# Attention's value projection moved ahead of attention as seven half-size block products

## The chip, the cores and the metric

The kernel runs on one core of a Trainium2 chip. Its time is the device time of one execution in microseconds (us), and lower is better. The engines are named as in the profile: PE is the matrix engine (PEld its weight loads), DVE the vector engine, ACT the scalar engine, POOL the GpSimd engine, and SP the queue that issues nearly all DMAs.

## The reference

A trunk of two layers works on a sequence of 1024 tokens of width 1024 in float32. The second layer mixes tokens by differential attention with 8 heads; cut to what matters here:

```python
q, k, v = jnp.split(hn @ w_qkv, 3, axis=-1)          # hn = rms_norm(h): 1024 x 1024; w_qkv: 1024 x 3072
q = rms_norm(q.reshape(b, s, 8, 2, 64), q_gain) * 64 ** -0.5
k = rms_norm(k.reshape(b, s, 8, 2, 64), k_gain)
v = v.reshape(b, s, 8, 128)
logits = einsum('bqhrd,bkhrd->bhrqk', q, k) - slopes * dist      # slopes[hd] = 2 ** -(hd + 1), causal mask
probs = softmax(logits)
o = einsum('bhqk,bkhe->bqhe', probs[:, :, 0] - lam * probs[:, :, 1], v)
h = h + (rms_norm(o, sub_gain) * (1 - lam_init)).reshape(b, s, 1024) @ w_out
```

The value projection is thus one product of 1024 x 1024 by 1024 x 1024. After attention come a wide MLP and a gated embedding, as in the first layer.

## The kernel before, in words

Matrix products keep float32 accuracy by splitting each operand into a high and a low part (`split`, L228 to L238: a cast on ACT at L230, a subtraction at L234) and multiplying three times (`mm3`, L206): high by high, high by low, low by high. So one product step of 128 contraction rows is three PE instructions.

The stages run in this order: the mixer of the first layer, an MLP, a gate called `ple`, then `attention`, then its output projection, a second MLP and a second gate, `ple_out`. In `mlp` and `ple_out` a large product is already done as seven products of half-size blocks with additions of the operands beside them. The inputs of attention are the 16 pairs of `hs`: the transposed activations times their norm's gain, high and low, for 8 slices of channels by two halves of 512 tokens. The norm's factor per token, `r`, is multiplied in later.

In `attention` PE work comes from two sources. The blocks: for each head `hd` and each block `b` of 128 queries (64 blocks in all) a `Block` makes logits (`qk`, against the keys `ks`), a DVE instruction that adds the distance bias `al` and takes the running minimum (L1132), an exponential on ACT (L1135), a combination of the two softmaxes on DVE (`combine`, L1141 to L1143), transposes (`tr`) copied back by ACT (`aT`, L1153), and the product with the values (`po`, L1160). The blocks are staggered: combination one block later, transposes and values two blocks later. The other source is the fill: a generator `fill` of projections. Each `next(fill)` emits one unit of 12 PE instructions, 128x256 each; a projection of a head's queries and keys has 16 units, half of one of a pair of heads' values has 8. That makes 128 units for queries and keys and 64 for values. 24 units come before the first block. The rest are spread over 264 calls of `pump`, four per block, by the table `MARKS` (call number, units by then): 168 units by call 226. Output projection parts (`tail`) follow from call 210 on.

Value units take weights through SP into `raw`, split them (the cast on ACT, the subtraction on POOL for projections) and leave the product through ACT (`proj_v`, L1049), which scales by `r` and writes a tile for two heads. For each head the queries are transposed and split by `put_q`: ACT writes the high part of one half of the partitions (L1091), DVE copies it to the other half (L1092) and makes the low part (L1093). The bias: slopes halve from head to head, so each block first halves its newest 128 columns of `al` on DVE (L1118).

A scheduler with a cost model of its own sets the order in which each engine gets its instructions; names, priorities and dependencies are what the code gives it.

Of the kernel before, what the change touches and what calls it, by code (L numbers as in the profile page):

```python
# [11 lines left out]
F32 = mybir.dt.float32  # L12
F32R = mybir.dt.float32r
AF = mybir.ActivationFunctionType
ALU = mybir.AluOpType
# [28 lines left out]
def f32(ap):  # L44
    return ap.bitcast(F32)
# [73 lines left out]
class Trunk:  # L119
# [581 lines left out]

    def ple_out(self, pT, acc, gain, wg, wpj, out):
        nc = self.nc
        o = out.rearrange("(t p) f -> p t f", p=P)
# [249 lines left out]

    def attn_consts(self, q_gain, k_gain, lam, sub_gain, lam_init):
        nc, cp = self.nc, self.cp
        qg = cp.tile([P, 1], F32, name="qg")
        kg = cp.tile([P, 1], F32, name="kg")  # L960
        for t, a in ((qg, q_gain), (kg, k_gain)):
            for i in range(2):
                nc.sync.dma_start(t[64 * i : 64 * (i + 1), :], a.rearrange("(p o) -> p o", o=1))
        nc.vector.tensor_scalar(kg, kg, 8.0, None, ALU.mult)
# [17 lines left out]
    def attention(self, w_qkv, w_out, gain_next, h_dram):  # L982

        nc = self.nc
        NB = NT
# [57 lines left out]
        def proj_v(pr, hf, out):  # L1043
            def evac(t2, ps):
                if len(out) == pr:
                    out.append(self.slot(f"A{pr % 2}", [P, NT, 256], F32, "v"))
                for i in range(2):
                    t = 2 * t2 + i
                    nc.scalar.activation(out[pr][:, t, :], ps[:, 256 * i : 256 * (i + 1)], AF.Copy, scale=r[t // 4][:, t % 4 : t % 4 + 1])  # L1049

            return proj(f"v{pr}", [w_qkv[:, 2 * D + pr * 256 : 2 * D + (pr + 1) * 256]], (2 * hf, 2 * hf + 1), evac)

        half = (slice(0, 64), slice(64, P))


# [11 lines left out]
        def begin(hd):  # L1067

            qk = qks[hd]

            ks = self.slot(f"A{2 + hd % 2}", [P, 2, S], F32R, "ks")

            def put_k(hf):
                pt = self.aux([P, HT], "tr", "tr")
                for t in range(4):
                    self.pe.transpose(pt[:, t * P : (t + 1) * P], qk[1][hf][:, t, :], self.ident)
                for r in range(2):
                    own, other = half[r], half[1 - r]
                    dst = ks[:, r, hf * HT : (hf + 1) * HT]
                    nc.scalar.activation(dst[own], pt[own], AF.Copy, scale=self.kg[own])  # L1080
                    nc.vector.scalar_tensor_tensor(dst[other], pt[own], self.kg[own], f32(dst[own]), ALU.mult, ALU.subtract)

            def put_q(b2):
                pt = self.aux([P, HT], "tr", "tr")
                for i in range(2):
                    self.pe.transpose(pt[:, i * P : (i + 1) * P], qk[0][b2 // 2][:, 2 * (b2 % 2) + i, :], self.ident)
                qh = self.slot(f"c{11 + b2 % 2}", [P, 2, 2 * P], F32R, "qh")
                ql = qlow[b2 % 2]
                for r in range(2):
                    own, other = half[r], half[1 - r]  # L1090
                    nc.scalar.activation(qh[own, r], pt[own, 0 : 2 * P], AF.Copy, scale=self.qg[own])  # L1091
                    nc.vector.tensor_copy(qh[other, r], f32(qh[own, r]))  # L1092
                    nc.vector.scalar_tensor_tensor(ql[own, r], pt[own, 0 : 2 * P], self.qg[own], f32(qh[own, r]), ALU.mult, ALU.subtract)  # L1093
                return qh, ql

            put_k(0)
            heads[hd] = [ks, put_k, put_q, put_q(0)]

        class Block:
# [12 lines left out]

            def logits(me, r):
                hd, b, n, nm, lg = me.hd, me.b, me.n, me.nm, me.lg[r]
                if r == 0:

                    new = al[:, (NB - 1 - b) * P : (NB - b) * P]
                    inst = nc.vector.tensor_scalar(new, new, 0.5, None, ALU.mult)  # L1118
                    if b:

                        self.pe.behind(inst, self.pe.mark)
# [4 lines left out]
                for c in range(nch):  # L1126
# [3 lines left out]
                    self.pe.matmul(ps[:, : k1 - k0], lhsT=ql[:, r, qs], rhs=ks[:, r, k0:k1], start=False, stop=True)  # L1130

                    nc.vector.tensor_tensor_reduce(  # L1132
                        out=lg[:, k0:k1], in0=ps[:, : k1 - k0], in1=al[:, u0 + k0 : u0 + k1], scale=-1.0,
                        scalar=3.0e38 if c == 0 else nm[:, r, 0:1], op0=ALU.add, op1=ALU.min, accum_out=nm[:, r, c : c + 1])
                nc.scalar.activation(lg[:, :n], lg[:, :n], AF.Exp, bias=nm[:, r, nch - 1 : nch], scale=-1.0, accum_out=me.sums[:, b, r : r + 1])  # L1135

# [77 lines left out]
        for hd in range(1, 8):  # L1214
            projs.append(proj_qk(hd, qks[hd]))
            if hd < 7:
                projs.append(proj_v((hd + 1) // 2, (hd + 1) % 2, vs))
        fill = self.stream(projs)
        for _ in range(24):
            next(fill)  # L1220
        begin(0)

        marks = [(0, 0), *MARKS]
# [2 lines left out]
        def pump():  # L1226
            i = state[0] = state[0] + 1
            for (i0, u0), (i1, u1) in zip(marks, marks[1:]):
                if i0 < i <= i1:
                    want = u0 + (u1 - u0) * (i - i0) / (i1 - i0)  # L1230
                    while state[1] < want:
                        next(fill)
                        state[1] += 1
            if i > TAIL and (state[1] < 168 or i % 4):
                next(tail, None)

        def tails():
            while state[1] < 160:
                yield
            for i in range(KA[0]):  # L1240
                fetch_o(0, i)
            while state[1] < 168:
# [11 lines left out]
        tail = tails()  # L1254
        blocks = []
        for g in range(8 * NB + 2):
            if g < 8 * NB:
# [849 lines left out]
def trunk(tc, x, p, ln_mix_e, w_in_e, gmlp_v_gain, gmlp_ws, gmlp_bs, gdn_conv, gdn_a_log, gdn_dt_bias, gdn_out_gain,  # L2107
          w_out_e, ln_mix_o, w_qkv_o, attn_q_gain, attn_k_gain, diff_lambda, attn_sub_gain, w_out_o, ln_mlp, w_mlp1,
          w_mlp2, ln_ple, w_ple_gate, w_ple_proj, masks, out):
    with ExitStack() as ctx:  # L2110
# [60 lines left out]
        for layer in range(2):  # L2171
# [23 lines left out]
            T.ple(pT, acc, w_ple_gate[0], w_ple_proj[0], gain[3], h_dram)  # L2195
            T.wide = ("mm",)
            T.attention(w_qkv_o[0], w_out_o[0], gain[4], h_dram)


# [39 lines left out]
```

## Time and profile before

| | before |
|---|---|
| timed runs, median (lowest to highest) | 2499.75 us (2499.11 to 2500.47) |
| profiled execution: its span, first to last instruction | 2498.9 us |
| PE, DVE, ACT, POOL busy | 2490.6, 1809.4, 1312.3, 285.6 us |
| the chain that ended last: on PE, on DVE | 96%, 2% |
| granted PE clock | 1.000 |

The page gives no other time of the profiled execution than its span, which is 0.85 us below the median of the timed runs. A row of grouped instructions reads: line, engine, operation, output tile <- input tiles, shape, count | busy us, mean ns of one | idle time of the engine before them and what ended it. The ends of PE's instructions are modelled and overlap, so PE's pace is read from the starts: a row of the chain gives a start, a length and a count. A row of stretches gives, for a stretch of the span, its length and each engine's busy time with the number of instructions.

### The profile page before, as it was taken

What the parts mean: (1) busy time and instruction counts of PE and PEld (TensorE: products, weight loads), DVE (VectorE), ACT (ScalarE), POOL (GpSimd) and SP (SyncE); (2) the same over time, 40 slices, a digit from 0 to 9 for tenths busy, and PEclk for the clock granted to TensorE, in tenths of its full rate; (3) what the DMA queues carried; (4) which work ended last, traced back from release to release, by engine and by line L of the source; (5) the groups of instructions that cost most, each with busy time, mean ns of one, the idle gap of its engine ahead of it and who ended that gap; (6) DMA issues with size and microseconds to landing.
All of it is one profiled execution on the core that took longest, in us unless ns stands there. A gap on an engine that the chain in (4) does not pass through costs nothing.

```text
span 2498.9 us, 39861 instructions
## 1 busy us (share of the span) xinstructions
PE 2490.6 (100%) x13897; PEld 2138.1 (86%) x13897; DVE 1809.4 (72%) x3542; ACT 1312.3 (53%) x2668; POOL 285.6 (11%) x267
## 2 busy tenths in 40 slices
PE   9999999999999999999999999999999999999999
PEld 7898998888888888888999999988888888888887
DVE  7868665787666877656577877777887656788586
ACT  6635473655555444544466666654654555445452
POOL 0211220000000000000444444310000000000000
PEclk9999999999999999999999999999999999999999
DMA  8464435567547756543211111366466548656651
GB/s 236 128 187 107 141 125 172 161 207 241 188 166 272 241 160 213 188 130 132 81 52 60 52 52 60 108 216 223 154 222 221 197 159 295 200 192 200 197 177 64
DMA packets 319506, 411.07 MB, mean 165 GB/s; under 512 B 46308, under 2 KB 182472, under 8 KB 319304
## 3 DMA queue, kind: packets, MB, share of 16 engines
q1 hardware_dynamic: 318744, 408.00, 50.6%
q8 instruction: 109, 1.79, 0.3%
q14 instruction: 93, 0.76, 0.1%
q10 hardware_dynamic: 560, 0.53, 0.1%
HBM read 296.21 MB, written 112.21 MB: 163 GB/s over the span
## 4 chain that ended last, share of the span: by engine, by line
PE 96%; DVE 2%; issue 1%; ACT 0%; DMA 0%; ACTq 0%; DVEq 0%
PE mm L80 84%; PE po L80 3%; PE qk L80 2%; PE aux L80 2%; PE tr L83 2%; DVE lg L1132 1%; DVE lg L1143 0%; DMA x<-in_x_dram 0%; PE pks L80 0%; PE pkq L80 0%; PE pkk L80 0%; PE pvn L80 0%; PE pgm L80 0%; PE pab L83 0%; PE pst L80 0%
## 5 line engine op out<-in xcount | busy, mean ns | idle before, releaser
L230 ACT CAST w<-raw 128x512 fp32r<-128x512 f32 x598 | 366.6, 617 | 463.7 <-PE mm L80 404.2
L80 PE MATMUL mm<-g,w 128*128 128x512 f32 x2592 | 601.6, 394 | 0.0
L80 PEld LDWEIGHTS mm<-g,w 128*128 128x128 f32 x2592 | 486.6, 188 | 113.9
L80 PE MATMUL mm<-hi,w 128*128 128x512 f32 x1728 | 554.5, 396 | 0.0
L80 PE MATMUL mm<-w,hi 128*128 128x256 f32 (+2 forms) x2528 | 507.2, 295 | 0.9 <-DVE k L1034 0.9
L234 DVE TENSOR_TENSOR w<-raw,w 128x512 fp32r<-128x512 f32 x534 | 366.8, 693 | 192.1 <-ACT w L230 180.3
L80 PEld LDWEIGHTS mm<-w,hi 128*128 128x128 f32 x2528 | 401.2, 188 | 13.8 <-issue 1.2
L80 PEld LDWEIGHTS mm<-hi,w 128*128 128x128 f32 x1728 | 324.4, 188 | 73.7 <-ACT u L386 0.4
L80 PE MATMUL mm<-w,lo 128*128 128x256 f32 (+2 forms) x1264 | 370.1, 294 | 0.0
L80 PE MATMUL mm<-lo,w 128*128 128x512 f32 x864 | 340.3, 394 | 0.0
L80 PE MATMUL mm<-t,w 128*128 128x512 f32 x1152 | 271.4, 394 | 0.0
L80 PEld LDWEIGHTS mm<-t,w 128*128 128x128 f32 x1152 | 216.4, 188 | 50.6
L80 PEld LDWEIGHTS mm<-w,lo 128*128 128x128 f32 x1264 | 238.1, 188 | 5.5
L80 PEld LDWEIGHTS mm<-lo,w 128*128 128x128 f32 x864 | 162.5, 188 | 36.2
L275 POOL TENSOR_TENSOR r<-ms,mhalf 128x4 f32<-128x4 f32 x12 | 14.1, 1173 | 1505.1 <-DVE ms L273 1474.5
L234 DVE TENSOR_TENSOR g<-graw,g 128x512 fp32r<-128x512 f32 x216 | 147.7, 686 | 6.6 <-DMA gd<-g 5.8
L230 ACT CAST g<-graw 128x512 fp32r<-128x512 f32 x216 | 132.6, 617 | 23.4 <-DMA gd<-g 7.3
L1135 ACT ACTIVATE lg<-lg,nm 128x256 f32<-128x256 f32 (+7 forms) x128 | 99.2, 776 | 69.1 <-DVE nm L1132 64.2
L370 ACT ACTIVATE g<-g 128x512 f32<-128x512 f32 x100 | 63.0, 631 | 79.5 <-DVE g L304 79.2
L1132 DVE CUSTOM_DVE_ANT_0 lg<-qk,al 128x512 f32<-128x512 f32 (+3 forms) x128 | 74.6, 589 | 36.9 <-PE qk L80 33.2
L234 POOL TENSOR_TENSOR w<-raw,w 128x512 fp32r<-128x512 f32 x64 | 84.1, 1335 | 76.2 <-ACT w L230 58.2
L80 PE MATMUL mm<-ohi,w 128*128 128x512 f32 x256 | 84.3, 400 | 0.0
(360 smaller groups left out, 3574.2 us busy)
## 6 DMA issues: line engine op xcount, KB each, us to landing
raw<-in_w_mlp_dram SPq DMA_DIRECT2D x352, 256.0 KB, 3.3
graw<-gd SPq DMA_DIRECT2D x224, 256.0 KB, 2.7
gd<-g SPq DMA_DIRECT2D x192, 256.0 KB, 3.4
raw<-in_w_ple_gate_dram SPq DMA_DIRECT2D x76, 256.0 KB, 3.5
acc<-h_dram SPq DMA_DIRECT2D x64, 256.0 KB, 4.4
keep<-in_w_mlp_dram SPq DMA_DIRECT2D x64, 256.0 KB, 4.8
raw<-in_w_in_e_dram SPq DMA_DIRECT2D x60, 256.0 KB, 3.6
h_dram<-acc SPq DMA_DIRECT2D x48, 256.0 KB, 3.3
```

Of the source, the lines that this page charges most:

```text
L80: self._next(self.engine.matmul(*a, **k))
L83: self._next(self.engine.transpose(*a, **k))
L230: inst = self.nc.scalar.copy(hi, src)
L234: inst = (lo_engine or self.nc.vector).tensor_tensor(lo, src, f32(hi), ALU.subtract)
L275: nc.gpsimd.tensor_tensor(r, ms, self.mhalf[:, 0:4], ALU.pow)
L370: nc.scalar.activation(g, src, AF.Relu)
L1132: nc.vector.tensor_tensor_reduce(out=lg[:, k0:k1], in0=ps[:, : k1 - k0], in1=al[:, u0 + k0 : u0 + k1], scale=-1.0, scalar=3.0e38 if c == 0 ...
L1135: nc.scalar.activation(lg[:, :n], lg[:, :n], AF.Exp, bias=nm[:, r, nch - 1 : nch], scale=-1.0, accum_out=me.sums[:, b, r : r + 1])
```

## The change

The value projection leaves the fill. A new function `values` runs between `ple` and `attention`. It treats activations and value weights as two by two blocks of 512 (`a11` to `a22` of `hs`, and `w_qkv`'s last 1024 columns) and makes seven products of 512x512x512 after Winograd: `s1` to `s4` are sums of activations, written over the residual stream `acc`, which is in DRAM by then; `t1` to `t4` are sums of weight blocks. Two sets of four PSUM banks, `x` and `y`, collect the products; ACT copies and DVE additions scale by `r` and combine them, and SP stores the results to `v_dram` in 32 pieces. `attention` reads them back as four tiles of two heads each: two before the first head, one each at blocks 18 and 34. The fill holds 128 units, 16 of them before the first block and 112 spread evenly to call 224, a half per call (before about 0.73). The subtractions for value weights, formerly POOL's, are DVE's in `values`.

Two smaller edits in `attention`: `al` is no longer halved; instead the queries' gain of head `hd` is multiplied by 2^(hd+1) and the DVE instruction's scale is -0.5^(hd+1). And ACT writes both halves of a query tile from PSUM; the copy on DVE is gone.

```diff
-MARKS = ((64, 50), (192, 144), (226, 168))
+MARKS = ((224, NQK),)
...
+    def values(self, acc, gain, w_qkv):
...
+        a11, a12, a22 = self.hs[0][0:4], self.hs[0][4:], self.hs[1][4:]
+        v_dram = self.dp.tile([NT, P, D], F32, name="v_dram")
...
+        def product(ps, a, b, new=False):
+            for k in R:
+                for q in R:
+                    self.mm3(ps[q], [y[:, q * P : (q + 1) * P] for y in a[k]], b[k], new and k == 0, k == 3, not new)
...
+        b11 = right(lambda k: raw(0, 0, k))
...
+            tt(t1[k], raw(0, 1, k), raw(0, 0, k), ALU.subtract)
...
+        product(x, a11, b11, True)
+        copies(u, x, 0)
+        b21 = right(lambda k: raw(1, 0, k))
+        for k in R:
+            tt(t2[k], t1[k], raw(1, 1, k), ALU.subtract)
+        product(y, a12, b21, True)
+        close(0, 0, y, u)
+
+        for k in R:
+            nc.scalar.activation(acc[k][1], acc[k][1], AF.Copy, scale=gain[:, k : k + 1])
+            scaled(acc[4 + k][1], 4 + k, 1, acc[k][1], ALU.add)
...
+        s2s = left(("A4", "A5"), s2)
+        t2s = right(lambda k: t2[k])
+        product(x, s2s, t2s)
+        copies(u, x, 0)
...
+        product(y, s1s, t1s, True)
+        copies(t, y, 1)
...
+        product(x, s3s, t3s)
+        close(1, 1, x, t)
...
+        product(y, s4s, b22)
+        close(0, 1, y, u)
...
+        product(x, a22, t4s)
+        close(1, 0, x)
...
-                    nc.scalar.activation(qh[own, r], pt[own, 0 : 2 * P], AF.Copy, scale=self.qg[own])
-                    nc.vector.tensor_copy(qh[other, r], f32(qh[own, r]))
+                    nc.scalar.activation(qh[own, r], pt[own, 0 : 2 * P], AF.Copy, scale=g)
+                    nc.scalar.activation(qh[other, r], pt[own, 0 : 2 * P], AF.Copy, scale=g)
...
-                    inst = nc.vector.tensor_scalar(new, new, 0.5, None, ALU.mult)
...
-        projs = [proj_v(0, 0, vs), proj_qk(0, qks[0]), proj_v(0, 1, vs)]
...
+        fill = self.stream([proj_qk(hd, qks[hd]) for hd in range(8)])
+        for _ in range(16):
             next(fill)
+        values(0)
+        values(1)
```

What stands in the queues differs at three places on which the steps below rest. First PE, behind the last product of `ple` (`aux<-phi`); `hi`, `lo` are the activations of attention, `w` weights, and `aux<-ones,sqs` sums the squares of the second half of the tokens. Before:

```order
L80 MATMUL aux_12167<-phi_8239,wpl_11315 128x512
L80 MATMUL mm_12266<-w_12244,hi_11712 128x256
L80 MATMUL mm_12266<-w_12245,hi_11712 128x256
L80 MATMUL mm_12266<-w_12244,lo_11713 128x256
...
L80 MATMUL aux_12216<-ones,sqs_11841 128x1 x4
```

After (the first row is again the last of `ple`, and `s` is the split `s2`):

```order
L81 MATMUL aux_12175<-phi_8247,wpl_11323 128x512
L81 MATMUL mm_12286<-w_12236,hi_11720 128x512
...
L81 MATMUL mm_12293<-w_12358,lo_11741 128x512
L81 MATMUL aux_12224<-ones,sqs_11849 128x1 x4
L81 MATMUL mm_12287<-w_12236,hi_11720 128x512
...
L81 MATMUL mm_12286<-w_12476,s_12466 128x512
```

Between the last row of `ple` and the sum of squares stand 73 instructions of 128x256 before, 54 of 128x512 now; 42 more of the first two products follow it, and then the third product, which needs `s2`.

Second DVE at the same time, from the last gate's product with `rb` (L671, now L672) to the last sum of squares (`sqs`). Before:

```order
L671 TENSOR_TENSOR t_12174<-mm_12125,rb_11402 128x512
L257 TENSOR_TENSOR sqs_11841<-sqs_11841,t_12164 128x512
L246 SCALAR_TENSOR_TENSOR lo_12209<-acc_8280,cols,hi_12208 128x512
L674 SCALAR_TENSOR_TENSOR t_12177<-t_12174,aux_12167 128x512
L675 SCALAR_TENSOR_TENSOR acc_8280<-t_12177,acc_8280 128x512
L257 TENSOR_TENSOR sqs_11841<-sqs_11841,t_12181 128x512
```

After (`raw` rows make `t3`, `acc` rows from L740 make `s1` to `s4`):

```order
L672 TENSOR_TENSOR t_12182<-mm_12133,rb_11410 128x512
L740 SCALAR_TENSOR_TENSOR acc_8285<-acc_8285,cols,acc_8288 128x512
L258 TENSOR_TENSOR sqs_11849<-sqs_11849,t_12172 128x512
L247 SCALAR_TENSOR_TENSOR lo_12217<-acc_8288,cols,hi_12216 128x512
L740 SCALAR_TENSOR_TENSOR acc_8285<-acc_8285,cols,acc_8288 128x512
L714 TENSOR_TENSOR raw_12666<-raw_12666,raw_12668 128x512
L740 SCALAR_TENSOR_TENSOR acc_8286<-acc_8286,cols,acc_8285 128x512
L675 SCALAR_TENSOR_TENSOR t_12185<-t_12182,aux_12175 128x512
...
L676 SCALAR_TENSOR_TENSOR acc_8288<-t_12185,acc_8288 128x512
...
L258 TENSOR_TENSOR sqs_11849<-sqs_11849,t_12189 128x512
```

Counted from the L674 (now L675) before the last but two to that last sum of squares, DVE had 18 instructions and has 42 now. Third ACT, where a new head begins (`ks` keys, `qh` queries, `lg` the exponentials). Before:

```order
L1080 ACTIVATE ks_16476<-tr_16477,kg 64x512
L1091 ACTIVATE qh_16489<-tr_16486,qg 64x256
L230 CAST w_16308<-raw_16306 128x512
L230 CAST w_16441<-raw_16439 128x512
L1080 ACTIVATE ks_16476<-tr_16477,kg 64x512
L230 CAST w_16591<-raw_16588 128x512
L1091 ACTIVATE qh_16489<-tr_16486,qg 64x256
```

After:

```order
L1188 ACTIVATE ks_16382<-tr_16383,kg 64x512
L1143 ACTIVATE t_16461<-mm_16318 128x512
L1200 ACTIVATE qh_16395<-tr_16392,qg 64x256
L1201 ACTIVATE qh_16395<-tr_16392,qg 64x256
L1237 ACTIVATE lg_12932,sums_15826<-lg_12932,nm_16402 128x1024
L1188 ACTIVATE ks_16382<-tr_16383,kg 64x512
L1200 ACTIVATE qh_16395<-tr_16392,qg 64x256
L1201 ACTIVATE qh_16395<-tr_16392,qg 64x256
```

The casts of weights moved elsewhere, two query copies came in, and an exponential stands between.

More of the change, by code (lines that the diff above doesn't have):

```diff
@@ L32 @@
 KA = (6,5)
[L33 removed]
+NQK = 112
+MARKS = ((224, NQK),)
 TAIL = 210
@@ L980, in attn_consts, with attention @@
         self.qg, self.kg, self.sg, self.nlam = qg, kg, sg, nl
-    def attention(self, w_qkv, w_out, gain_next, h_dram):
+    def attention(self, w_qkv, v_dram, w_out, gain_next, h_dram):
         nc = self.nc
@@ L1211, in attention, with values @@
         qks, vs, os = [[] for _ in range(8)], [], [[] for _ in range(8)]
-        projs = [proj_v(0, 0, vs), proj_qk(0, qks[0]), proj_v(0, 1, vs)]
[L1214 to L1219, printed above, removed]
+        def values(pr):
+            vs.append(self.slot(f"A{pr % 2}", [P, NT, 256], F32, "v"))
+            nc.sync.dma_start(vs[pr], v_dram[:, :, pr * 256 : (pr + 1) * 256].rearrange("t p f -> p t f"))
+        fill = self.stream([proj_qk(hd, qks[hd]) for hd in range(8)])
+        for _ in range(16):
             next(fill)
+        values(0)
+        values(1)
         begin(0)
@@ L1256, in attention @@
         for g in range(8 * NB + 2):
+            if g in (2 * NB + 2, 4 * NB + 2):
+                values(g // (2 * NB) + 1)
             if g < 8 * NB:
@@ L2195, in trunk @@
             T.ple(pT, acc, w_ple_gate[0], w_ple_proj[0], gain[3], h_dram)
+            T.wide = ("mm", "tr", "aux", "sc")
+            v_dram = T.values(acc, gain[3], w_qkv_o[0])
             T.wide = ("mm",)
-            T.attention(w_qkv_o[0], w_out_o[0], gain[4], h_dram)
+            T.attention(w_qkv_o[0], v_dram, w_out_o[0], gain[4], h_dram)
 _INS = ['x', 'p', 'ln_mix_e', 'w_in_e', 'gmlp_v_gain', 'gmlp_ws', 'gmlp_bs', 'gdn_conv', 'gdn_a_log', 'gdn_dt_bias',
```

95 lines of the change are left out of this document (76 added, 19 removed).

## Prediction

> **What bounds the kernel now.** I read the page's busy times and its chain first, then the chain piece by piece around attention, then busy time by stretches, then the groups of instructions that the change touches.
>
> ```profile
> PE 2490.6 (100%) x13897; PEld 2138.1 (86%) x13897; DVE 1809.4 (72%) x3542; ACT 1312.3 (53%) x2668; POOL 285.6 (11%) x267
> PE 96%; DVE 2%; issue 1%; ACT 0%; DMA 0%; ACTq 0%; DVEq 0%
> ```
>
> PE is busy all the time and carries 96% of the chain. But its ends are modelled, so its pace has to be read from the chain's pieces (start, length, what, how many):
>
> ```profile
> 480.85 296.11 PE mm L80 x1278
> 1203.94 8.60 PE mm L80 x73
> 1213.33 19.83 PE mm L80 x167
> 2417.90 12.00 PE mm L80 x52
> ```
>
> An instruction of 128x512 (the MLP at 480.85) takes 296.11 / 1278 = 0.2317 us, one of 128x256 (the projections at 1213.33) 19.83 / 167 = 0.1187 us. Attention's blocks run from 1245 to about 1720. Four of its heads, one per stretch, with PE, PEld, DVE, ACT and POOL in that order, and all waits of PE that the trace finds there:
>
> ```profile
> 1354.00:1413.00 59.00, 58.39 (x471) 56.74 (x472) 47.00 (x131) 37.78 (x94) 25.51 (x24) 1.00 0.17 55
> 1413.00:1471.00 58.00, 57.63 (x464) 55.74 (x464) 46.36 (x128) 37.85 (x95) 26.00 (x24) 1.00 0.18 56
> 1471.00:1527.00 56.00, 56.00 (x458) 54.89 (x457) 42.66 (x127) 37.06 (x91) 23.62 (x23) 1.00 0.17 53
> 1527.00:1583.00 56.00, 56.00 (x459) 54.89 (x458) 41.84 (x128) 37.89 (x95) 24.70 (x26) 1.00 0.17 56
> PE mm L80 <- DVE k L1034: 0.9, 2, 0.5
> PE tr L83 <- DVE ks L1081: 0.6, 1, 0.6
> PE tr L83 <- DVE ql L1093: 0.2, 1, 0.2
> ```
>
> A head lasts 229 / 4 = 57.3 us, with DVE busy 177.9 / 4 = 44.5 us (78%) and ACT 150.6 / 4 = 37.6 us (66%). PE's waits are 1.7 us in all. So attention is bound by PE, with DVE next.
>
> **The change, part by part.** The profiled span is 2498.9 us, 0.85 below the median of the runs; I add up against the span and put the 0.85 back.
>
> *PE's work.* 64 value units of 12 instructions go: 768 x 0.1187 = 91.2 us. Seven products of 4 x 4 x 3 instructions come: 336 x 0.2317 = 77.8 us. Sum: -13.4 us, if PE is as closely fed as now.
>
> *The start of the products.* Here PE may wait. DVE around the end of the first gate (start, length):
>
> ```profile
> 1195.72 0.69 DVE L674 SCALAR_TENSOR_TENSOR t<-t,aux 128x512 f32<-128x512 f32 x1 [4.25 <-PE aux L80]
> 1209.31 0.69 DVE L675 SCALAR_TENSOR_TENSOR acc<-t,acc 128x512 f32<-128x512 f32 x1
> 1210.70 0.69 DVE L257 TENSOR_TENSOR sqs<-sqs,t 128x512 f32<-128x512 f32 x1 [0.70 <-ACT t L256]
> 2420.00:2440.00 20.00, 20.00 (x88) 16.25 (x87) 20.00 (x33) 14.93 (x27) 0.00 (x0) 1.00 0.16 53
> ```
>
> Now the last sum of squares ends at 1211.4, before PE has finished its first 73 value instructions at 1203.94 + 8.60 = 1212.5: no wait. In the new order 42 DVE instructions stand from the one at 1195.72 to that sum. The last row (a stretch of `ple_out`, where DVE is full) has 33 in 20.00 us, 0.606 each, so the sum ends at 1195.72 + 25.5 = 1221.2. PE has 54 instructions ahead of it, 12.5 us, and stands there from 1216.4: a wait of 4.8 us, with the 42 instructions behind it and then the third product queued up, and nothing else on PE to fill it. Lower bound: 0, if the scheduler's order hides more than I count. Upper: instructions that depend on each other start 0.71 apart (1208.60 to 1209.31 in the same view), which gives 29.8 us for 42 and a wait of 9.1. I take 4.8, since few of the 42 depend on their neighbour.
>
> *The rest of the products.* 44 splits, 16 sums of weights, 16 of activations and 12 closings are 88 DVE instructions, or 53 us at 0.606, beside 77.8 us of PE. The same stretch of `ple_out` says what a full DVE does to a product in seven parts: at 2417.90 PE runs 52 instructions in 12.00 us, 0.231 each. So it is hidden; without that cover every further microsecond of DVE would be one of PE. The loads (36 of 256 KB) and stores (32) go through SP and are named by this row:
>
> ```profile
> raw<-in_w_qkv_o_dram SPq DMA_DIRECT2D x8, 256.0 KB, 2.9
> ```
>
> At 2.9 us from issue to landing, the last store and the 1 MB reads behind it end within some 10 us of the last product; the first product with values needs them some 40 us after that, behind 16 units (22.8 us) and the first blocks. No cost. SP holds two later reads until heads 0 and 1, or 2 and 3, are done; they are wanted 16 blocks later.
>
> *Attention's other engines.* What goes and comes, by groups of the stage:
>
> ```profile
> L230 ACT CAST w<-raw 128x512 fp32r<-128x512 f32 x79 | 48.3, 618 | 22.5 <-PE mm L80 18.5 <-issue 2.0 <-DMA res<-h_dram 0.8
> L1091 ACT ACTIVATE qh<-tr,qg 64x256 fp32r<-64x256 f32 x64 | 29.8, 466 | 18.2 <-DVE ql L1093 10.1 <-PE tr L83 7.4
> L1092 DVE CAST qh<-qh 64x256 fp32r<-64x256 f32 x64 | 28.8, 450 | 7.7 <-ACT qh L1091 6.4
> L1118 DVE TENSOR_SCALAR al<-al 128x128 f32<-128x128 f32 x63 | 16.5, 263 | 0.3
> L1049 ACT ACTIVATE v<-mm,r 128x256 f32<-128x256 f32 x32 | 13.4, 472 | 0.5 <-PE mm L80 0.4
> L1092 DVE CAST qh<-qh x64: 279/290/1383, 1234.5 to 1682.8; 64x256 fp32r<-64x256 f32 x64
> ```
>
> Per head, PE loses 96 instructions, 11.4 us: 57.3 - 11.4 = 45.9 us. DVE loses 8 x 0.263 + 8 x 0.450 = 5.7 us: 38.8 us, 85% of the new head. ACT loses 32 / 7 casts and as many evacuations, 4.6 x (0.618 + 0.472) = 5.0 us, and gains 8 x 0.466 = 3.7 us: 36.3 us, 79%. PE stays the fullest engine, but with less fill between the steps of a block (0.5 units a call instead of 0.73), some waits must show. From nothing (it can gain 1.7 us where today's waits go with the edits on DVE) up to the price of the second rival; I take 0.3 us a head, 2 us in all, near the row of today's waits, because PE holds no more than that with DVE at 80% (47.00 of 59.00).
>
> The copy of the queries is the place for the skill's rules. The last row gives its shortest, median and longest time: 290 ns at the median, 1383 at most, on DVE; the same write costs 466 ns on ACT. The Trainium skill, "ScalarE: Activation LUTs", section "Rules for kernel authors", says that plain arithmetic belongs on VectorE and not on ScalarE. That speaks against this edit, and median against median the trace agrees: 176 ns lost per copy; by that rule the sum would rest on ACT, and come out as the second rival's 2506.8. Its "SBUF — State Buffer", section "Who interferes with whom", says that a copy of this kind is shut out for the whole length of a GpSimd instruction. The 1383 ns fit that, and POOL's value splits leave attention too; by that rule DVE would come out below 38.8 us, which speaks against the second rival.
>
> Sum: -13.4 + 4.8 + 2.0 = -6.6 us; 2498.9 - 6.6 + 0.85 = 2493.1.
>
> **The rivals.** First, *more of the gain stays*: PE's wait at the start is hidden and attention's present waits vanish: -13.4 - 1.7 = -15.1, 2484.7. For it: PE is fed almost without a gap in all other stages. Against: the 42 DVE instructions.
>
> Second, *ACT and DVE become a ring that is slower than PE* (the slower side). In each block the exponential needs the minimum from DVE, the combination needs the exponential, and the next block's second logits overwrite what the combination reads. The trace of the logits' tile:
>
> ```profile
> DVE nm L1132: 64.2, 53
> ACT aT L1153: 30.2, 33
> ```
>
> ACT waited 64.2 us for minima and 30.2 us for transposes, 8.0 and 3.8 us a head. Today that is slack. If it does not shrink with the head, ACT needs 36.3 + 11.8 = 48.1 us a head against PE's 45.9: 2.2 us x 7 = 15.6 us. Then -13.4 + 4.8 + 15.6 = +7.0, 2506.8. It decides from 1.2 us of waits a head on (8.6 us of gain left, over 7 heads). For it: two more copies per pair of blocks stand on ACT ahead of an exponential, and three engines lie within 21% of each other. Against: these waits are mostly waits for work that PE had not yet delivered, and a faster PE delivers sooner.
>
> Third, *nothing left to measure*: the wait at the start is 9.1 us and attention's is 3 us: -1.3, 2498.5. The start is the place, and DVE's dependent pace the reason.
>
> **How the numbers follow.** A measurement of this kernel can tell about 0.2%, 5 us, from no change: under 2494.8 is faster, over 2504.7 slower. My forecast has 0.36, the first rival 0.15, the second 0.27, the third 0.22. Of the forecast's 0.36 about 0.03 spill into no change. So faster 0.48, the same 0.25, slower 0.27. The likeliest time is 2493.1. Its own range, with 0 to 9.1 us at the start and -1.7 to 3 in attention, is 2484.7 to 2498.5. With the second rival, whose 2.2 us a head may be 3 (21 us, 2512), the range that should hold 8 times in 10 is 2485 to 2512.
>
> **What would show it.** Right: a wait of PE of some 5 us just before the ones times squares, 12 us behind the first gate; 336 instructions of 128x512 that start 0.232 us apart; heads of 46 to 47 us in attention, with DVE near 85% and ACT near 79%. Wrong: heads over 47.5 us, with PE's transposes and logits waiting for DVE or ACT, which would mean that fill was what hid their chain; or a wait of PE over 10 us at the start; or PE waiting for `v_dram`.

## The result, and the profile after

The changed kernel takes 2524.13 us (median of 4 runs, 2521.94 to 2524.44). The kernel before, on the same chip, takes 2500.11 us (4 runs, 2499.11 to 2503.03). The ratio is 1.0093, with a 95% interval from 1.0082 to 1.0105: slower by some 24 us, where I had forecast 7 us faster and a range that ended at 2512. The profiled execution after has a span of 2522.2 us, 23.3 more than the span before.

The page after, busy times and chain:

```profile
PE 2492.6 (99%) x13465; PEld 2114.7 (84%) x13465; DVE 1813.1 (72%) x3510; ACT 1346.0 (53%) x2732; POOL 245.6 (10%) x235
PE 92%; DVE 4%; ACT 2%; issue 1%; DMA 0%; POOL 0%; SPq 0%; DVEq 0%; ACTq 0%
```

PE has 432 instructions less and is not less busy by the page, because the ends of its instructions are modelled. The chain says more: ACT now has 2% of it, and DVE 4% instead of 2%.

The start of the products. First PE's waits from 1195 to 1319 us, all that the trace finds; then stretches, as in the prediction (length, PE, PEld, DVE, ACT, POOL, granted clock); then three pieces of the chain:

```profile
PE aux L81 <- DVE sqs L258: 6.2, 1, 6.2
```

```profile
1215.00:1221.70 6.70, 0.50 (x3) 0.07 (x1) 6.67 (x12) 2.12 (x4) 0.00 (x0) 0.90 0.22 79
1221.70:1223.60 1.90, 1.89 (x9) 1.90 (x10) 1.90 (x4) 0.00 (x1) 0.00 (x0) 0.50 0.00 0
1223.60:1228.00 4.40, 4.40 (x12) 3.50 (x13) 4.36 (x10) 2.38 (x4) 1.50 (x1) 0.59 0.11 18
1228.00:1235.00 7.00, 7.00 (x32) 5.67 (x31) 7.00 (x13) 6.99 (x14) 0.00 (x0) 1.00 0.24 74
```

```profile
1221.05 0.61 DVE sqs L258
1221.71 1.87 PE aux L81 x8
1223.58 84.07 PE mm L81 x426
```

PE stands for 6.2 us in front of the ones times squares, and then works at a granted clock of 0.50 to 0.59 until about 1227. From there on it is closely fed: the 426 instructions are 282 of the products and 144 of the first projection, 282 x 0.2317 + 144 x 0.1187 = 82.4 us of work in 84.07.

The first exponential of attention, before and after:

```profile
1245.75 0.40 ACT L1135 ACTIVATE lg<-lg,nm 128x128 f32<-128x128 f32 x1 [1.74 <-DVE nm L1132]
```

```profile
1319.34 0.40 ACT L1237 ACTIVATE lg<-lg,nm 128x128 f32<-128x128 f32 x1 [1.30 <-DVE nm L1234]
```

So 73.6 us are lost by then. The stores of the products play no part in it: the trace has 16 of 256 KB, not 32 as the text ahead and the prediction say, and none of PE's waits up to 1740 us is for a DMA. From there to the end the kernel after takes 1202.9 us, before 1253.1: only 50.3 us come back. Five heads, from the 17th exponential to the 97th (16 make a head; the 17th is the first of head 1, and where two heads overlap the 97th can still belong to the head that ends); stretches of before and of after:

```profile
1295.80:1583.40 287.60, 286.27 (x2318) 279.09 (x2317) 220.59 (x639) 187.33 (x461) 125.65 (x120) 1.00 0.17 55
```

```profile
1362.50:1617.40 254.90, 242.84 (x1862) 228.10 (x1861) 188.60 (x561) 182.83 (x461) 97.26 (x98) 0.99 0.15 51
```

A head, counted as 16 exponentials, lasts 254.9 / 5 = 51.0 us, before 287.6 / 5 = 57.5. By the count of its instructions PE lost 11.4 us of work per head, and the head became 6.5 us shorter. DVE is busy for 37.7 us of it and ACT for 36.6 us, 74% and 72%, less full than before in the case of DVE (77%). Nothing is saturated, and the heads are still 5 us longer than the 45.9 us of PE work forecast for them. The page counts 254.9 - 242.84 = 12.1 us of the five heads as idle on PE, 2.4 us a head. The rest of the 5 us is not seen as waits. A part of it can be hidden by the modelled ends: below, an instruction of 128x256 is shown as 0.28 us long, while in a closely fed stream they start 0.1187 us apart. A small part is the clock (last section). PE's waits in these five heads (the four largest groups), and what ACT waits for (groups of 3 us and more):

```profile
PE tr L84 <- DVE ks L1189: 5.0, 4, 1.2
PE mm L81 <- DVE k L1152: 3.1, 5, 0.9
PE qk L81 <- DVE nm L1234: 1.0, 4, 0.5
PE qk L81 <- DVE ql L1202: 0.8, 3, 0.3
...
ACT lg L1237 <- DVE nm L1234: 33.5, 27, 2.9
ACT aT L1255 <- PE tr L84: 17.2, 20, 2.0
ACT qh L1200 <- PE tr L84: 8.0, 5, 2.3
ACT ou L1293 <- PE tr L84: 7.2, 7, 1.4
```

PE waits at many places for DVE, ACT waits for DVE and for PE. One place shows how it looks; PE between two heads:

```profile
1459.19 0.28 PE L81 MATMUL mm<-w,lo 128*128 128x256 f32 x1
1459.31 0.22 PE L81 MATMUL qk<-ks,qh 128*128 128x128 f32 x1
1459.80 0.33 PE L81 MATMUL qk<-ks,ql 128*128 128x128 f32 x1 [0.27 <-DVE ql L1202]
1461.37 0.63 PE L84 MATMUL tr<-ident,lg 128*128 128x128 f32 x4 [1.25 <-DVE ks L1189]
1462.07 0.39 PE L81 MATMUL qk<-ks,qh 128*128 128x256 f32 x1
1462.30 0.28 PE L81 MATMUL qk<-ks,ql 128*128 128x256 f32 x1
1462.69 0.61 PE L84 MATMUL tr<-ident,lg 128*128 128x128 f32 x2
1463.09 1.92 PE L81 MATMUL po<-v,aT 128*128 128x128 f32 x8
...
1465.98 0.55 PE L81 MATMUL mm<-w,hi 128*128 128x256 f32 x2
```

Up to 1459.2 PE worked through fill (`mm<-w`). Then come only steps of the blocks, some of which wait for DVE's keys and queries, and the next fill starts at 1465.98. In the kernel before, 24 units a head stood between such steps; now there are 16. Taken from the PE rows of the five heads, before has 21 stretches of more than 1.5 us without an instruction of the fill, the longest 2.5 us and 39 us in all; after has 30, the longest 6.5 us and 105 us in all.

### The profile page after: what moved, and what is told of

The parts are those of the page before. It is cut to its first block, busy times and chain, and to the rows that moved or that the text cites. A ratio compares the mean times of both kernels' runs of the same rounds, so it can differ in the third digit from the quotient of the medians.

```text
span 2522.2 us, 39013 instructions
## 1 busy us (share of the span) xinstructions
PE 2492.6 (99%) x13465; PEld 2114.7 (84%) x13465; DVE 1813.1 (72%) x3510; ACT 1346.0 (53%) x2732; POOL 245.6 (10%) x235
## 3 DMA queue, kind: packets, MB, share of 16 engines
q1 hardware_dynamic: 321688, 417.43, 51.5%
## 4 chain that ended last, share of the span: by engine, by line
PE 92%; DVE 4%; ACT 2%; issue 1%; DMA 0%; POOL 0%; SPq 0%; DVEq 0%; ACTq 0%
PE mm L81 81%; PE po L81 2%; PE aux L81 2%; PE qk L81 2%; PE tr L84 2%; DVE lg L1234 1%; ACT lg L1237 1%; ACT qh L1201 0%; ACT qh L1200 0%; PE pks L81 0%; PE pkq L81 0%; PE pkk L81 0%; PE pvn L81 0%; PE pgm L81 0%; DVE w L235 0%
## 5 line engine op out<-in xcount | busy, mean ns | idle before, releaser
L231 ACT CAST w<-raw 128x512 fp32r<-128x512 f32 x582 | 357.2, 618 | 475.2 <-PE mm L81 431.9
L235 DVE TENSOR_TENSOR w<-raw,w 128x512 fp32r<-128x512 f32 (+1 forms) x550 | 376.0, 690 | 199.7 <-ACT w L231 191.3
L81 PE MATMUL mm<-w,hi 128*128 128x256 f32 (+2 forms) x2112 | 439.0, 303 | 4.8 <-DVE k L1152 4.8
L81 PEld LDWEIGHTS mm<-w,hi 128*128 128x128 f32 x2112 | 338.4, 189 | 24.5 <-DVE k L1152 6.3
L81 PE MATMUL mm<-w,lo 128*128 128x256 f32 (+2 forms) x1056 | 317.4, 301 | 0.0
L81 PEld LDWEIGHTS mm<-t,w 128*128 128x128 f32 x1152 | 216.5, 188 | 50.7
L81 PEld LDWEIGHTS mm<-w,lo 128*128 128x128 f32 x1056 | 199.3, 189 | 8.0
L1237 ACT ACTIVATE lg<-lg,nm 128x1024 f32<-128x1024 f32 (+7 forms) x128 | 99.5, 778 | 59.1 <-DVE nm L1234 58.6
L81 PE MATMUL mm<-ahi,w 128*128 128x512 f32 x256 | 83.1, 400 | 0.2 <-ACT ahi L1785 0.2
```

Of the source, the lines that this page charges most:

```text
L81: self._next(self.engine.matmul(*a, **k))
L231: inst = self.nc.scalar.copy(hi, src)
L235: inst = (lo_engine or self.nc.vector).tensor_tensor(lo, src, f32(hi), ALU.subtract)
```

## The experiments

Each is an edit of the changed kernel, unless it says otherwise. A head is a fifth of the time from the 17th to the 97th exponential, as above. Each ratio is to runs of the kernel before made beside that run (medians 2499.98 to 2500.61 us).

| run | median us | ratio to before, 95% interval | a head, us |
|---|---|---|---|
| before | 2500.11 | | 57.5 |
| the changed kernel | 2524.13 | 1.0082 to 1.0105 | 51.0 |
| e1_dve_copy | 2522.35 | 1.0072 to 1.0102 | 50.7 |
| e2_bias_back | 2516.66 | 1.0048 to 1.0078 | 49.5 |
| e3_edits_only | 2496.42 | 0.9975 to 0.9994 | 57.4 |
| e4_values_only | 2521.46 | 1.0067 to 1.0100 | 50.5 |
| e5_late_sums | 2519.13 | 1.0059 to 1.0089 | 50.7 |
| e6_dummy | 2539.54 | 1.0141 to 1.0171 | 53.1 |
| e7_hold_fill | 2526.27 | 1.0085 to 1.0118 | 52.2 |
| e8_half_fill | 2472.10 | 0.9874 to 0.9904 | 45.1 |
| e9_short_combine | 2520.72 | 1.0065 to 1.0095 | 51.5 |
| e10_short_exp | 2499.77 | 0.9986 to 1.0005 | 47.4 |
| e11_late_bias | 2509.55 | 1.0023 to 1.0049 | 49.5 |
| e12_slopes_only | 2497.90 | 0.9980 to 0.9999 | 57.2 |
| e13_no_squares | 2512.08 | 1.0031 to 1.0065 | 49.7 |
| e14_act_more | 2523.93 | 1.0081 to 1.0111 | (see below) |
| e15_aT_dve | 2524.70 | 1.0084 to 1.0115 | 51.3 |
| e16_late_aT | 2519.74 | 1.0064 to 1.0094 | 51.3 |
| e17_act_more2 | 2525.77 | 1.0082 to 1.0115 | 51.5 |
| e18_exp_no_min | 2516.90 | 1.0049 to 1.0079 | 49.8 |

### Which edit is it?

The first four take the change apart: the queries' copies back on DVE (e1), the halving of the bias back (e2), the two small edits without the values (e3, an edit of before), the values without the small edits (e4).

```diff
-                    nc.scalar.activation(qh[other, r], pt[own, 0 : 2 * P], AF.Copy, scale=g)
+                    nc.vector.tensor_copy(qh[other, r], f32(qh[own, r]))
```

```diff
+                if r == 0:
+                    new = al[:, (NB - 1 - b) * P : (NB - b) * P]
+                    inst = nc.vector.tensor_scalar(new, new, 0.5, None, ALU.mult)
...
-                        out=lg[:, k0:k1], in0=ps[:, : k1 - k0], in1=al[:, u0 + k0 : u0 + k1], scale=-0.5 ** (hd + 1),
+                        out=lg[:, k0:k1], in0=ps[:, : k1 - k0], in1=al[:, u0 + k0 : u0 + k1], scale=-1.0,
```

> The changed kernel with one edit undone: the second half of a query tile is again copied by DVE from the first half, not written by ACT. Theory A (lost cover: the blocks' steps on DVE and ACT are now slower than PE's work, because the value units that filled the gaps between them are gone): the ring of DVE and ACT has one step more on DVE and one less on ACT, heads stay at 50 to 52 us, 2519 to 2530 us. Theory B (the copies on ACT themselves lengthen the heads, since in the trace DVE's ql waits 13.3 us in five heads for ACT's qh): heads fall to 46 or 47 us, seven of them give back 4 to 5 us each, 2489 to 2497 us.

> The changed kernel with the other small edit undone: each block halves its newest 128 columns of the bias on DVE again (8 instructions of 0.26 us a head), and the scale is -1. Theory A: DVE is a part of the ring, so its 2.1 us a head come back in part or in full, 2526 to 2539 us. Theory B (only the ACT copies matter): no change, 2522 to 2526 us.

> The kernel before with the two small edits alone (bias slopes in the queries' gain, queries' copies on ACT); the values stay in the fill. Theory A: PE has fill enough to cover either order, so 2496 to 2501 us, heads as before at 57 us. Theory B: the ACT copies lengthen the heads here too, by 3 to 5 us each, 2515 to 2530 us.

> The values alone: the changed kernel with both small edits undone. Theory A: as long as the changed kernel or longer, heads 51 to 54 us, 2524 to 2550 us, since the small edits only took work off DVE. Theory B: heads 46 to 48 us, 2489 to 2505 us.

The values alone cost 21 us (e4). The small edits alone gain 3.6 us on the kernel before (e3); the bias slopes alone gain 2.6 (e12). Theory B has fallen: e1 has its copies on DVE and heads of 50.7 us. Theory A's own numbers hold for e1 and e3, but for e4 the time is 2.5 us below its range, and its expectation for e2 has fallen: 2.2 us a head more on DVE made the kernel 7.5 us faster, and its heads last by turns about 48 and 52 us. DVE's load is not the price. The scheduler orders all of attention anew after any edit, and kernels with the same PE work have heads between 49.5 and 52.2 us. So a difference of a microsecond a head between two of these runs can be order alone.

> The kernel before with the bias slopes in the queries' gain alone; the queries' copies stay on DVE and the values in the fill. The two small edits together gave 2496.4 us. If what they gave is DVE's 2.1 us a head of bias, this alone gives 2496 to 2498 us; if it is the move of the copies to ACT, 2499 to 2501 us.

At 2497.90 it lies in the first expectation, and the move of the copies adds some 1 us at most. That the gain comes from DVE's shorter work is not shown: of the 3.6 us of e3 only 0.5 arise in the five heads (287.1 us against 287.6), 2.6 before them, and a new order is a rival.

### What is the wait at the start worth?

```diff
+        product(x, s2s, t2s)
+        for q in R:
+            self.pe.matmul(y[3][:, q : q + 1], lhsT=self.sqs[1][:, q * P : (q + 1) * P], rhs=self.ones[:, 0:1], start=True, stop=True)
...
+        self.take_hs(1, ms, rows=False)
```

> The changed kernel with the second half's norm taken later: the ones times squares are summed in the midst of the third product, in a PSUM bank that is free there, since their factor is first needed after the fourth product. If the wait of 6.35 us before them and the low clock behind it (0.50 to 0.59 in the next 7 us, some 3 us) are lost to that order alone, PE goes on to the third product without standing and 6 to 9 us come back: 2515 to 2518 us. If DVE's work itself is the limit there, PE stands before the third product's operands instead, and 0 to 3 us come back: 2521 to 2525 us.

The 6.2 us are gone. PE's waits from 1200 to 1300 us, and the stretch in which it stands now:

```profile
PE mm L81 <- ACT s L231: 2.2, 1, 2.2
```

```profile
1235.00:1245.00 10.00, 7.83 (x23) 5.87 (x22) 8.40 (x16) 6.28 (x12) 0.78 (x1) 0.66 0.24 73
```

PE reaches operands of a later product 2.2 us early, and its clock falls there instead. The first exponential comes at 1316.4 us, 2.9 us sooner; the other 2 us of the gain arise behind it. Beside the bias edit the same move gives 7.1 us (e11 against e2). At 2519.13 us the run lies between its two expectations: the order is worth 3 to 6 us, and PE then stands before later operands, as the second one said.

> The best of the changed kernels put together: the late sum of squares and the bias halved on DVE as before. If the two gains (5.0 and 7.5 us against the changed kernel) add, 2511 to 2513 us, still slower than before. If either was a chance of the order in attention, 2514 to 2520 us.

At 2509.55 us the run is below both expectations: the gains add, and some 2 us more come that I can't place. With the values early this is the best that I found, still 9 us slower than before.

### Is a head bound by PE or by its chain?

Add idle fill (e6), leave out half of the fill (e8), hold the fill back in PE's order (e7):

```diff
+                        for _ in range(4):
+                            self.pe.matmul(ps[:, 256 * i : 256 * (i + 1)], lhsT=hs[h][0][0][:, c], rhs=w.at(0)[0], start=True, stop=False, skip_group_check=True)
```

```diff
                         for k in range(KT):
-                            self.mm3(ps[:, 256 * i : 256 * (i + 1)], [x[:, c] for x in hs[h][k]], w.at(k), k == 0, k == KT - 1)
+                            if k % 2 == 0:
+                              self.mm3(ps[:, 256 * i : 256 * (i + 1)], [x[:, c] for x in hs[h][k]], w.at(k), k == 0, k == KT - 2)
```

```diff
+        self.pe.start(2)
         def pump():
+            self.pe.slot()
...
+                    self.pe.fill = True
                     while state[1] < want:
```

> The changed kernel with 4 idle PE instructions of 128x256 more in front of each half bank of the projections (their sum is overwritten): 32 a head, 3.8 us of PE work, 30 us over eight heads, of which 26 lie in attention. Theory A (heads are bound by a chain of DVE, ACT and PE steps that leaves PE standing for some 5 us a head): the extra work fits in the waits, 2525 to 2540 us, heads 51 to 53 us. Theory C (heads are bound by PE's own stream: its instructions in their order, whatever stands beside them): the work comes on top, 2550 to 2556 us, heads near 54.5 us.

> The changed kernel with every second contraction step of the queries' and keys' projections left out (half of their PE instructions; the same number of units, evacuations and blocks): 8 x 96 = 768 instructions of 0.1187 us less, 91 us, of which 11.4 us a head lie in seven heads. Theory A: the chain sets the heads' time, so they fall only to 47 to 51 us, and the whole kernel by 11 us (head 0's projection) plus 0 to 28 us. Theory C: PE's work sets it, heads fall to 39 or 40 us, and the whole by 85 us or more.

> The changed kernel with the fill held back in PE's order: a projection's instructions must stand behind the blocks' instructions of two pump calls earlier, so that they no longer run 2 to 4 units ahead. Theory D (order: the scheduler has spent the fill early and nothing is left to cover the waits that the chip really has): heads fall to 46 to 48 us, 2493 to 2505 us. Theory A (the chain's own length): heads stay at 50 to 52 us, 2520 to 2530 us.

With idle fill the time (2539.54) is at the upper end of theory A's range and the heads (53.1) just above it. With half the fill neither theory holds: the heads fall to 45.1, between A's 47 and C's 40, and the whole to 2472.1, 52 us less, between A's 39 and C's 85. Stretches of five heads, of the run with idle fill and of the one with half the fill:

```profile
1367.10:1632.80 265.70, 256.51 (x2040) 246.28 (x2039) 197.41 (x564) 183.74 (x462) 96.95 (x100) 1.00 0.15 51
```

```profile
1350.60:1576.10 225.50, 193.09 (x1379) 171.46 (x1378) 188.83 (x563) 185.20 (x462) 96.96 (x98) 0.98 0.20 66
```

DVE (37.7 to 39.5 us a head) and ACT (36.6 to 37.0) do the same work in all three kernels, only the fill differs. A head of before has 57.3 us of PE work, 34.2 of it fill (288 x 0.1187), so the blocks' own is 23.1:

| fill of a head, us of PE | fill and blocks | measured | left over | of it idle on PE by the page |
|---|---|---|---|---|
| 11.4 (e8) | 34.5 | 45.1 | 10.6 | 6.5 |
| 22.8 (the changed kernel) | 45.9 | 51.0 | 5.1 | 2.4 |
| 26.6 (e6) | 49.7 | 53.1 | 3.4 | 1.8 |
| 34.2 (before) | 57.3 | 57.5 | 0.2 | 0.3 |

This is the main result. Each microsecond of fill that leaves a head brings back 0.42 to 0.48 us in which PE is not fed. Of 11.4 us taken out, 6.5 are gained. The sizes carry an error of about a microsecond a head, since each edit also brought a new order. Holding the fill back in this way (e7) does not help: heads last 52.2 us, a little longer, and theory D's 46 to 48 are not reached. But it does not rule out order as a part of the 5.1 us: in e7, too, stretches of up to 5.8 us have no fill, and other orders of the same work gave heads of 49.5 (e2).

### Which part of the chain?

Shorten one step: the combination on DVE (e9), the exponentials on ACT (e10); and the exponentials in full, but without their minimum (e18), which e10 had dropped as well:

```diff
-nc.vector.scalar_tensor_tensor(me.lg[0][:, :n], me.lg[1][:, :n], rs, me.lg[0][:, :n], ALU.mult, ALU.add)
+nc.vector.scalar_tensor_tensor(me.lg[0][:, :P], me.lg[1][:, :P], rs, me.lg[0][:, :P], ALU.mult, ALU.add)
```

```diff
-nc.scalar.activation(lg[:, :n], lg[:, :n], AF.Exp, bias=nm[:, r, nch - 1 : nch], scale=-1.0, accum_out=me.sums[:, b, r : r + 1])
+nc.scalar.activation(lg[:, n - P : n], lg[:, n - P : n], AF.Exp, scale=0.0, accum_out=me.sums[:, b, r : r + 1])
```

> The changed kernel with the combination of the two softmaxes on DVE done for the first 128 columns of a block only (the other columns stay as they are): by the durations of the profile after, 33.6 us of these instructions in five heads become 40 x 0.348 = 13.9, 3.9 us of DVE a head less, at the same place of the chain and in the same number of steps. Theory A1 (PE waits for the length of DVE's steps in the chain): heads fall by 2 to 4 us, the whole by 14 to 28 us, 2496 to 2510 us. Theory A2 (PE waits for the handovers between the engines and for the order, not for DVE's time): heads fall by under 1 us, 2517 to 2526 us.

> The changed kernel with the exponentials on ACT done for a block's last 128 columns only, and on zeros instead of the shifted logits: 61.5 us of these instructions in five heads become 80 x 0.402 = 32.2, 5.9 us of ACT a head less, at the same place of the chain. Theory A1, for ACT as well: heads fall by 3 to 5 us, 2489 to 2503 us. Theory A2: by under 1 us, 2517 to 2526 us. If the one of the two engines counts and the other not, this run and the one with the short combination differ by 10 us or more.

> The changed kernel with exponentials of full length on zeros, without the minimum as their bias: the same work on ACT, and no wait for the minimum's own read-out behind DVE's instruction (0.08 us). If the 24 us of the short exponentials came from their length, this one stays at 2517 to 2526 us; if they came from the wait that was dropped, it falls to 2500 to 2506 us.

DVE's 3.9 us a head (3.1 by its busy time) give 3.4 us (2520.7), which a new order can give as well, and heads of 51.5. ACT's 5.9 us give 24.4 us, the whole loss; 7.2 of that come with the dropped minimum (e18, as much as a new order can give), and some 17 with the length, the new order included. Five heads with short exponentials, and all of PE's waits there:

```profile
1358.70:1595.60 236.90, 234.87 (x1886) 227.18 (x1885) 193.84 (x564) 152.46 (x460) 98.28 (x99) 1.00 0.16 55
```

```profile
PE mm L81 <- DVE k L1152: 0.8, 2, 0.5
PE po L81 <- DVE nm L1234: 0.4, 1, 0.4
PE qk L81 <- DVE nm L1234: 0.4, 1, 0.4
PE mm L81 <- ACT aT L1255: 0.3, 1, 0.3
```

PE is fed again. Is it ACT's load, then? Take the blocks' squares from ACT (e13), put idle work behind each exponential (e14, e17), move the transposes' copies to DVE (e15; e16 with the late sums):

```diff
-                nc.scalar.activation(sq, po, AF.Square, accum_out=me.osq[:, b : b + 1])
+                nc.gpsimd.memset(me.osq[:, b : b + 1], 1.0)
```

```diff
+                nc.scalar.activation(spare, al[:, :P], AF.Copy, scale=me.sums[:, b, r : r + 1])
```

```diff
-nc.scalar.copy(me.aT[c][:, : (k1 - k0) * P], pt[:, : (k1 - k0) * P])
+nc.vector.tensor_copy(me.aT[c][:, : (k1 - k0) * P], pt[:, : (k1 - k0) * P])
```

> The changed kernel without the squares of the blocks' results on ACT (their sums are set to one): in the profile after, 40 x (0.274 + 0.199) = 18.9 us in five heads, 3.8 us of ACT a head, which nothing in the block's chain waits for. Theory L (ACT's load: whatever stands in ACT's queue delays the exponentials behind it): heads fall by 2 to 3 us, 2500 to 2510 us. Theory P (the exponentials' own length between two steps of DVE): heads fall by under 1 us, 2517 to 2525 us.

> The changed kernel with an idle copy of 128x128 on ACT behind each exponential, which nobody waits for: 16 a head, by the row of the copies of this size 0.273 us each, 4.4 us of ACT a head more. Theory L: heads get longer by 2 to 4 us, 2538 to 2552 us. Theory P: by under 1 us, 2522 to 2531 us.

> The changed kernel with the copies of the transposes (aT) on DVE and not on ACT: 29.1 us in five heads, 5.8 us a head, go from ACT (43.9 us of a head then 38) to DVE (43 then near 49 of 51). Theory L with DVE's time for free, as the short combination had it: heads fall by 3 to 4 us, 2496 to 2505 us. Theory P: heads stay, 2519 to 2530 us. If DVE counts as soon as it is full: heads get longer than 52 us, over 2530 us.

> The transposes' copies on DVE together with the late sum of squares: 4 to 6 us below the run with the copies on DVE alone, since the late sum gave 5.0 us by itself. By theory L 2491 to 2500 us, which would be a version as fast as the kernel before or faster; by theory P 2514 to 2525 us.

> The changed kernel with an idle instruction of 128x128 on ACT behind each exponential, scaled by that exponential's sum so that it cannot be issued earlier; nobody waits for it. 16 a head at some 0.28 us, 4.5 us of ACT a head more, against 3.8 us less in the run without squares (12 us gained) and 5.9 us less in the run with short exponentials (24 us gained). Theory L (ACT's load): heads get longer by 2 to 4 us, 2538 to 2552 us. Theory P (the exponentials' own length and place): by under 1 us, 2522 to 2531 us.

e14 says nothing on ACT's load. Its copies had no tie to the exponentials (`nc.scalar.copy(spare, al[:, :P])`), and the trace of the tile shows where the scheduler put them (shortest, median and longest time in ns, first and last start):

```profile
L1239 ACT COPY spare<-al x128: 278/298/301, 1087.6 to 1165.4; 128x128 f32<-128x128 f32 x128
```

All of them ran before attention, which is then as in the changed kernel. e17 ties them to the sums; its copies, its five heads and ACT's largest waits there:

```profile
L1239 ACT ACTIVATE spare<-al,sums x128: 386/402/423, 1320.5 to 1739.4; 128x128 f32<-128x128 f32 x128
```

```profile
1362.60:1620.10 257.50, 245.97 (x1879) 229.39 (x1878) 187.65 (x563) 211.21 (x542) 100.80 (x98) 0.99 0.15 50
```

```profile
ACT lg L1238 <- DVE nm L1235: 21.9, 23, 1.6
ACT aT L1257 <- PE tr L84: 10.7, 19, 1.1
```

ACT has 16 x 0.402 = 6.4 us a head more (5.7 by its busy time), and the heads are 0.5 us longer, the whole kernel 1.6 us. The new work went into ACT's waits, which fell from 33.5 to 21.9 us and from 17.2 to 10.7. So theory L has fallen in the form in which I put it: more work on ACT does not lengthen the heads. e15 says less than it seems: its heads stay as theory P said, but while ACT's busy time fell from 36.6 to 32.9 us a head, DVE's rose from 37.7 to 42.7, and ACT's waits for the minima rose from 33.5 to 62.9 us in five heads. With the late sums e16 is 5.0 us below e15, as expected.

It is not shown that work taken from ACT counts only where it is an exponential. e13 remains without an answer: its 12 us lie between the two expectations, a new order alone has given 7, and per microsecond of ACT taken away (12 us for 3.8 a head) it gains three quarters of what the short exponentials do (24.4 us for 5.9), though no step of a block's chain takes the squares' result. What is shown is that the shortened exponentials bring the heads from 51.0 to 47.4 us, more than any new order did. That they do it by the time that steps of a block take one behind the other is an argument.

## Why the prediction was wrong

**PE's work, -13.4 us.** Right: the products are closely fed behind the start.

**The start of the products, 4.8 us.** The mechanism and nearly the time were right. The sum of squares ended at 1221.7 us, forecast 1221.2; PE stood for 6.2 us. What the step lacked is the clock: 8 instructions of one column took 1.87 us (0.81 before), and the 426 behind them lost 84.07 - 82.4 = 1.7 us. Together that is some 9 us, less the 1.1 us by which PE reached the first value product sooner (1202.84, before 1203.94). It is near the upper bound, but not by DVE's dependent pace.

**The rest of the products and the DMAs, nothing.** Right: from 1195 to 1319 us the trace finds no other wait of PE, and none for `v_dram` behind that.

**DVE 38.8 and ACT 36.3 us a head.** Right in size: 37.7 and 36.6.

**Attention's waits, 0.3 us a head.** This is the step that failed: "I take 0.3 us a head, 2 us in all, near the row of today's waits, because PE holds no more than that with DVE at 80%". The runs show 5.1 us a head, and e6 and e8 show it grow and shrink with the fill. The prediction had named this sign of being wrong itself: heads over 47.5 us, with PE's transposes and logits waiting for DVE or ACT. The row of today's waits was measured with 34.2 us of fill in a head. It said how much of the chain's latency was left over once the fill had covered it, not how long the chain is. I took busy shares for slack: neither DVE at 74% nor ACT at 72% is full, and PE is still not fed. A price for the lost cover was to be had only by a kernel with less fill.

**The sum.** By the first exponential 73.6 us are lost: 77.8 for the products, less the 11.4 of eight value units that stood there, make 66.4; some 7 remain for the start. Behind it 56 units, 79.8 us of PE work, are gone and 50.3 us come back. 73.6 - 50.3 = 23.3. The missing 29.5 us are lost in attention, where I had put 2.

**The rivals.** The second had the right side, the right place and the observation that counts, that waits that hardly shrink lengthen the head: in the same five heads ACT's waits for minima went from 7.3 us a head to 6.7, and those for transposes stayed at 3.4 (its 8.0 and 3.8 were an eighth of the sums over all heads). Its price, 2.2 us a head, was still too small by more than half, and its mechanism is not what happened. It added ACT's busy time and its waits up to a pace; e17 shows that ACT can take 6.4 us more in a head that is only 0.5 us longer. Against it I wrote that "a faster PE delivers sooner". It does so only as far as PE does not itself wait, and in the rows above it waits for DVE's answers. The first rival had the wrong side. The third had the start nearly right (9.1 us), but put attention at 3 us in all, nearly as far off as my own 2.

**The copies and DVE's time.** That plain arithmetic belongs on VectorE, as the Trainium skill says in "ScalarE: Activation LUTs", section "Rules for kernel authors", decided nothing here: with the copies on DVE the changed kernel takes 2522.4 us, with them on ACT 2524.1; in the kernel before, on ACT together with the slopes 2496.4, slopes alone 2497.9, each within what a new order can do. The lower DVE time that the Trainium skill's "SBUF — State Buffer", section "Who interferes with whom", let me expect did come: 37.7 us a head, not 38.8, and 38.6 in e3, where the value splits are still on POOL. The combination of 896 columns took 1868 ns on the mean before and 1152 after. No gain came of it.

**What stays open.** That shorter exponentials count and a shorter combination, which stands between them and the transposes, does not, is measured and not explained. How much of the 5.1 us is the order in which the fill is spent is open too. Nor did I find an order of attention that hides its chain with 16 units a head.

## What to carry to other kernels

Fill that covers a chain of short steps between engines is not only work: here each microsecond of it taken away gave back 0.57 (6.5 of 11.4), so moving 80 us of it out for 66 us of other work was a loss, though it is less work in all. Before moving fill, make a kernel that leaves out half of it and read what the stage then takes; busy shares, and the waits seen while the fill is there, do not tell. Of this change the part worth keeping is the small edits on the kernel before: 2496.42 us against 2500.01 (ratio 0.9985, 0.9975 to 0.9994), the version that beats both kernels, by 0.15%.

## What the runs showed of the hardware

The granted clock of PE fell here after short pauses, too. Behind the waits between two heads quoted above, stretches of the kernel after:

```profile
1459.30:1463.00 3.70, 2.00 (x12) 1.33 (x11) 3.57 (x11) 2.41 (x5) 1.84 (x2) 0.97 0.00 0
1463.00:1465.40 2.40, 2.40 (x13) 2.40 (x12) 1.94 (x6) 1.55 (x5) 0.00 (x0) 0.50 0.00 0
1465.40:1470.00 4.60, 4.60 (x39) 4.60 (x38) 2.26 (x11) 2.07 (x7) 0.00 (x0) 0.92 0.00 0
```

By the page PE was busy for 2.0 of 3.7 us, with no wait longer than 1.25, and then ran at 0.50 for 2.4 us: eight products with the values took 1.92 us there. The Trainium skill, "TensorE: Matmul & The Clock Gate", section "What's actually happening", says that half the rate follows a whole window of about 3.4 us without work. The 6.2 us at the start of the products agree with that; this place does not, and the measurement decides. In the run with the fill held back the mean clock of five heads was 0.97 and of the changed kernel 0.99, before 1.00. By estimate (1% of 51 us) half a microsecond of the 5.1 a head is this.
